# Pacing the sums in smaller transfers, gating a retention head slice by slice, and splitting one gate's weight earlier

## The chip, the cores and the metric

The kernel runs on one core of one Trainium2 chip. The metric is device time in microseconds for one execution of the whole program; lower is better. Before: 2340.71 us, the median of three timed runs. TensorE is the matrix engine, VectorE (DVE in the profile) and ScalarE (ACT) work on its results and on the weights, GpSimd (POOL) does small things and issues one kind of DMA, SyncE (SP) issues the loads of weights.

## What is computed

The reference is a trunk of two layers (512 frames, width 1024, float32). Cut to what matters:

```python
for i in range(DEPTH):                                   # 2 layers
    h = rmsnorm(x, norm1_g[i])
    z = h @ w_in[i] + b_in[i]                            # mLSTM q,k,v,o,i,f; retention q,k,v,g; gates gm, gr
    hm  = mlstm(conv_swish(q), conv_swish(k), v, i, f)   # 4 heads of 256
    y_m = sigmoid(o) * head_layernorm(hm)
    hr  = retention(rope(rq), rope(rk), rv)              # 4 heads, keys of 256, values of 512
    y_r = silu(rg) * head_layernorm(hr)
    merged = sigmoid(gm) * (y_m @ w_bm[i]) + sigmoid(gr) * (y_r @ w_br[i])
    x = x + merged @ w_out[i]
    x = x + square(relu(rmsnorm(x) @ w_ff1[i] + b_ff1[i])) @ w_ff2[i] + b_ff2[i]
    x = x + sigmoid(rmsnorm(x) @ w_pe_gate[i]) * (p[i] @ w_pe[i])
return rmsnorm(x, final_g)
```

## The kernel before, in words

**Units.** All products with weights are a list of 290 units, written out by hand (`unit_list`), 145 for each layer. A T8 unit makes 128 output columns from all eight 128-row blocks of the input (24 matmuls, the weight tile is 128x1024). A V unit is a quarter of a value projection. A PAIR unit makes 256 columns and a WIDE unit 1024 by a seven-product scheme (P1 to P7, in place of eight) on quarter matrices. Layer by layer the list goes: mLSTM (T8 and V), WIDE `rv0`, four T8 of `w_bm`, PAIRs of `rqk0` (tiles `r0brq`, `r0brk`) and of the gate `gm`, WIDE `rw0` and `rv2`, PAIRs of `rqk2`, T8 of `w_br`, WIDE `rw2`, PAIRs of the gate `gr` (tiles `gr0` to `gr3`) between T8 of `w_br`, T8 of `w_out`, then the channel block: T8 of `w_ff1` with PAIRs of `w_ff2` (tiles `o00` to `o33`: block, then pair), then the embedding. Every float32 product is three matmuls: each operand is split into a high part (fp32r) and the low rest, and high by high, low by high and high by low are added.

**Weights.** SyncE loads a weight tile `wr` (four raw buffers, `RAWS`); ScalarE copies it to the high half `wh` and VectorE subtracts to get the low half `wl` (`split`, lines 284 and 285). `prep_next` does this two pieces ahead of use (`LOOK`), and `in_order` keeps the order of the loads and that of the splits. The instructions of each engine run in one fixed order, which a scheduler derives from the program's order and from priorities (`tc.high_priority`). Of a PAIR's weight the pieces are A (`B11`, `t1`), C (`B22`, `t3`), B (`B21`) and D; B's second half is formed on VectorE (line 428) and D from B (line 431).

**Sums.** The seven-product scheme needs sums of weight blocks: `t1` and `t3`, and for WIDE units `t2` and `t4`. They are made ahead of time by DMA alone: GpSimd issues a copy DRAM to DRAM and later an adding one (`step`, line 332). `steps` is the list of all of them. A step has 256 KB in a group of PAIRs (`wpairs`) and 512 KB in a WIDE group (`wwide`: `rv0`, `rw0`, `rv2`, `rw2`). The pace is a credit that starts at -12: each unit adds `SHARE * t - load` (`TIME`: 5.45 and 1.5 for a T8 or V, 9.9 and 3.9 for a PAIR, 5.45 and 2.7 for each two turns of a WIDE), a step takes `STEP` (twice that for 512 KB), and `pace` issues one step where the credit is not negative. Every DMA of a step waits for the matmul that was last in the program when it was issued. `pace` is called at the start of each unit, in the middle of a T8, after each product of a PAIR, and at each second turn of a WIDE unit. A group must be made before its pieces are loaded.

**Retention heads.** `r_attend` runs `attend` (four row slices of 128 frames, each evacuated by ScalarE into `num`, line 801), then the statistics of all four slices (`head_stats`, lines 809 and 810), then `hv`, the power of the variance, on GpSimd (lines 1104 and 1105). `r_gate` of a slice scales the gate by `hv` on ScalarE (line 1143) and multiplies it with the centred slice on VectorE (line 1144). Heads 0 and 2 are gated in the middle of the WIDE unit that makes the gates (`r_gates`); heads 1 and 3 in a loop over the four slices after `r_attend`. `r_out` transposes the gated head on TensorE (line 821, tiles `ot`). `flush` runs the last product (P4) of the PAIR before, which is put off (`later`); P4 writes into the bank that P7's eviction (line 577) frees.

**The mLSTM gate.** `gm_tile(c)` makes a tile of the gate `gm` in a T8 unit (tiles `bgm`); `gm_tile(2)`, weight columns from `CGM + 2 * P`, stands between the output gates of head 0 and the transposes of head 0. `xn_tile` forms the normalised input (`xn`, a high and a low half) for all later units, the first of which is the T8 of head 2 (tiles `m2z`).

Of the kernel before, what the change touches and what calls it, by code (L numbers as in the profile page):

```python
# [35 lines left out]
F32 = mybir.dt.float32  # L36
# [6 lines left out]
P = 128  # L43
T = 512
NT = T // P
# [58 lines left out]
TURNS += [(x, u) for x in ("P7", "P3", "P4") for u in range(2)]  # L104
HALVES = [(WIDE[x][0], u) for x, u in TURNS]

STEP, SHARE = 1.13, 0.73
TIME = {"PAIR": (9.9, 3.9), "WIDE": (5.45, 2.7)}


# [9 lines left out]
def is_wide(g):  # L120
    return g[1][:2] in ("rv", "rw")
# [112 lines left out]
def build(ctx, tc, ins, out):  # L234
# [74 lines left out]
    def flat(a):  # L309
        return a.rearrange("a p q -> (a p q)").rearrange("(r w) -> r w", r=P)  # L310

    def sum_steps():

        out = []
        for g, v in groups().items():
            n = 2 if is_wide(g) else len(v)
            for p in range(n + 1):
                out += [(g, x, 0, p) for x in ("t1", "t3") if p < n]
                out += [(g, x, 1, p - 1) for x in ("t1", "t3") if p]
            out += [(g, x, a, p) for x in LATE if x in MADE_OF(g) for a in range(2) for p in range(n)]  # L320
        return out

    steps = sum_steps()
    made = {}

    def step():
        g, x, a, p = steps[at["step"]]
        at["step"] += 1
        at["credit"] -= STEP * (2 if is_wide(g) else 1)
        made[g, p] = made.get((g, p), 0) + 1  # L330
        kw = {"accum_op": OP.add} if a else {}
        dma = gp.dma_start(flat(block(g, x)[p:p + 1]), flat(block(g, MADE[x][a])[p:p + 1]), max_dma_last_dim=4096,
                           **kw)

        tc.add_manual_dep(dma.ins, cur["mm"].ins.name, SYNC, reason="pace of the sums")

# [3 lines left out]

    def tick(kind=None):
        t, load = TIME.get(kind, (5.45, 1.5))
        at["credit"] += SHARE * t - load
        pace()

    def next_unit():
# [47 lines left out]
    def prep_next():  # L394
# [15 lines left out]
        if gates:  # L410
            z = out_[0]
            gp.memset(z.bitcast(F32), 0.0)
            z = z.rearrange("p (k g c) -> p k g c", g=4, c=32)
            split(r[:, 0:64].rearrange("p (k g c) -> p k g c", g=2, c=H), z[:, :, 0:2, 0:H], z[:, :, 2:4, 0:H])
        elif x == 0:
            with tc.high_priority(AHEAD if n < 10 and units[n][0] == "V" else 0):
                for c in halves(n):
                    in_order("prep", *split(r[:, c], *[a[:, c] for a in out_]))
        else:
            in_order("prep", *split(r[:, :w], *out_))  # L420
# [96 lines left out]
    def run_wide(name, act, done, mid=None):  # L517
# [4 lines left out]
        for x, u in TURNS:  # L522
# [23 lines left out]
            if u:  # L546
                for t in range(2):
                    done(x, t, bank[b][t])

    def ahead():  # L550

        return tc.high_priority(AHEAD)

    def pair_tiles(name, act, consume, y=None):

        y = y or [tmp(f"{name}y{d}") for d in range(2)]
        a, b = slice(0, S), slice(S, T)

        def done(x, o):
            with ahead():  # L560
                evict(x, o)
            if x == "P4":
                consume(y)

        def evict(x, o):
            if x == "P1":
                ac.activation(y[0][:, b], o, AF.Copy)
            elif x == "P5":
                ac.activation(y[1][:, a], o, AF.Copy)
            elif x == "P2":  # L570
                ve.tensor_tensor(y[0][:, b], o, y[0][:, b], OP.add)
            elif x == "P6":
                ac.activation(y[1][:, b], o, AF.Copy)
            elif x == "P3":
                ve.tensor_tensor(y[1][:, b], o, y[1][:, b], OP.add)
            elif x == "P7":
                ve.tensor_tensor(y[1][:, a], o, y[1][:, a], OP.add)
            else:
                ac.activation(y[0][:, a], o, AF.Copy)

        run_pair(name, act, done)
# [209 lines left out]
            off += w  # L791
        return ph, pl, offs

    def attend(nm, pt, vh, vl, c0, n, num):
        ph, pl, offs = pt
        for j in range(NT):
            o = ps(f"{nm}a{j}")
# [3 lines left out]
            ac.activation(num[:, j, :], o[:, :n], AF.Copy)  # L801
            if j == 0:
                flush()

    def head_stats(nm, num, dv):
        st = cols.tile([P, NT, 6], F32, name=f"{nm}st", tag="st")
# [130 lines left out]
    for i in range(L):  # L937
# [157 lines left out]
            nc.scalar.dma_start(dg, ins["decay"][h])  # L1095
            return scores(f"l{i}r{h}", qk[0], qk[1], qk[2], qk[3], lambda a: dg[:, 0:T - a * P])

        def r_attend(h, pt, vv):
            nm = f"l{i}r{h}"
            num = cur["low"].tile([P, NT, 512], F32, name=f"{nm}num", tag="num")  # L1100
            attend(nm, pt, vv[0], vv[1], 0, 512, num)
            mv = head_stats(nm, num, 512)
            hv = cols.tile([P, NT], F32, name=f"{nm}hv", tag="hv")
            gp.tensor_scalar(hv, mv[:, :, 1], EPS, None, OP.add)
            gp.tensor_tensor(hv, hv, nhalf, OP.pow)
            return num, mv, hv

        def r_gates(h, norm, mid):

# [221 lines left out]
        g = r_gates(0, num, lambda: rv_split(vv))  # L1331
        yr = acts(cur["br"], f"l{i}yr0")
        r_out(0, num[0], yr)
        num = r_attend(1, pt, vv)
        for j in range(NT):
            r_gate(num, g, j)
        vv = rv_vals(2, lambda: r_out(1, num[0], yr))
        qk = r_qk(2)

# [14 lines left out]
        g = r_gates(2, num, lambda: rv_split(vv))  # L1354
        yr = acts(cur["br"], f"l{i}yr1")
        r_out(2, num[0], yr)
        num = r_attend(3, pt, vv)
        for j in range(NT):
            r_gate(num, g, j)
        mh, ml = [], []  # L1360
        gr = {}

        def gr_gates(p):
            def consume(g):
                for d in range(2):
                    ac.activation(g[d], g[d], AF.Sigmoid, bias=bcol(i, "bgr", 2 * p + d), scale=SIGN[d])
                    gr[2 * p + d] = g[d]

            pair_tiles(f"l{i}gr{p}", xs, consume)

        gr_gates(0)
        r_out(3, num[0], yr)
        for c in range(KT):
            if c and c % 2 == 0:
# [355 lines left out]
```

## Time and profile before

| what | value |
|---|---|
| timed runs, median (lowest to highest) | 2340.71 us (2340.2 to 2340.83) |
| the profiled execution | 2335.82 us |
| its span, first to last instruction | 2334.1 us |
| granted TensorE clock, mean | 0.998 |
| busy: TensorE, VectorE, ScalarE, GpSimd | 99%, 73%, 52%, 17% |
| DMA: mean rate; share of queue q0 (GpSimd's, the sums) and of q1 (SyncE's, the loads) | 181 GB/s; 26.0% and 34.0% |

The durations in the profile belong to the one profiled execution. Its own time is 1.7 us over its span and 4.9 us under the median of the timed runs. A row of waits tells which engine stood idle before which line and what released it; a small wait on TensorE moves everything behind it.

### The profile page before, as it was taken

The page shows a single profiled execution, that of the slowest core. Times are in us where ns is not written, and L with a number is a line of the kernel's source. Part 1 is how long each engine was busy: PE and PEld are TensorE (multiplying, and loading weights), DVE is VectorE, ACT ScalarE, POOL GpSimd, SP SyncE. Part 2 cuts the span into 40 slices and gives each one's busy share as a digit, 9 for nine tenths or more (in the row PEclk, how much of TensorE's full clock was granted, in tenths as well). Part 3 has the DMA queues.
Part 4 walks back from the last instruction along what each step waited for, and adds up shares of the span by engine and source line. Part 5 has one row for each costly group of instructions (what it writes and reads, how often), then busy time and mean ns, then how long its engine had stood idle before and what let it go on. Part 6 is the DMA issues. An engine that isn't in the chain of part 4 may idle for free.

```text
span 2334.1 us, 34266 instructions
## 1 busy us (share of the span) xinstructions
PE 2311.7 (99%) x12992; PEld 2019.8 (87%) x12992; DVE 1709.6 (73%) x2594; ACT 1217.2 (52%) x1731; POOL 398.3 (17%) x618
## 2 busy tenths in 40 slices
PE   9999999999999999999999999999999999999998
PEld 8888889888888888899888888988888988998997
DVE  7878767886765577678778777778767656776785
ACT  6756544644554445445557564445446445445464
POOL 3122111111124312111422222200000020000012
PEclk9999999999999999999999999999999999999999
DMA  6667877777788787787786668945444443433441
GB/s 219 165 178 194 233 218 207 211 223 217 203 243 250 190 229 185 213 221 195 209 229 165 163 162 244 257 148 174 143 148 153 149 154 98 127 109 95 136 122 55
DMA packets 152328, 422.13 MB, mean 181 GB/s; under 512 B 19089, under 2 KB 22545, under 8 KB 152161
## 3 DMA queue, kind: packets, MB, share of 16 engines
q1 hardware_dynamic: 97504, 257.99, 34.0%
q0 software_dynamic: 39248, 134.51, 26.0%
q10 hardware_dynamic: 15408, 27.43, 3.4%
q8 instruction: 102, 1.67, 0.3%
q14 instruction: 66, 0.53, 0.1%
HBM read 400.97 MB, written 140.51 MB: 232 GB/s over the span
## 4 chain that ended last, share of the span: by engine, by line
PE 87%; DVE 5%; issue 3%; DMA 2%; ACT 1%; POOL 1%; SPq 0%; DVEq 0%; ACTq 0%; POOLq 0%
PE l1f L449 2%; PE l0f L449 2%; PE l0f L450 2%; PE l1f L450 2%; PE l1f L451 2%; PE l0f L451 2%; PE l0br L449 1%; PE l1br L449 1%; PE l0br L450 1%; PE l1br L450 1%; PE l1br L451 1%; PE l0br L451 1%; DMA wr<-s8t 1%; PE l0pg L449 1%; PE l1bm L449 1%
## 5 line engine op out<-in xcount | busy, mean ns | idle before, releaser
L284 ACT ACTIVATE wh<-wr 128x1024 fp32r<-128x1024 f32 (+1 forms) x223 | 231.3, 1044 | 261.3 <-issue 62.7
L285 DVE TENSOR_TENSOR wl<-wr,wh 128x1024 fp32r<-128x1024 f32 (+1 forms) x221 | 272.4, 1234 | 49.6 <-ACT wh L284 49.3
L284 ACT ACTIVATE wh_B<-wr 128x1024 fp32r<-128x1024 f32 x108 | 114.4, 1060 | 175.9 <-PE l0br L450 15.7
L285 DVE TENSOR_TENSOR wl_B<-wr,wh_B 128x1024 fp32r<-128x1024 f32 x108 | 131.9, 1222 | 53.8 <-ACT wh_B L284 53.5
L449 PE MATMUL l1f<-l1n2h,wh 128*128 128x512 f32 x256 | 99.8, 390 | 0.0
L449 PE MATMUL l0f<-l0n2h,wh 128*128 128x512 f32 x256 | 99.8, 390 | 0.0
L451 PE MATMUL l1f<-l1n2h,wl 128*128 128x512 f32 x256 | 99.7, 389 | 0.0
L451 PE MATMUL l0f<-l0n2h,wl 128*128 128x512 f32 x256 | 99.6, 389 | 0.0
L450 PE MATMUL l0f<-l0n2l,wh 128*128 128x512 f32 x256 | 99.6, 389 | 0.0
L450 PE MATMUL l1f<-l1n2l,wh 128*128 128x512 f32 x256 | 99.6, 389 | 0.0
L284 ACT ACTIVATE wh_t<-wr 128x1024 fp32r<-128x1024 f32 x56 | 59.4, 1060 | 72.0 <-PE l0g2va L544 6.0
L284 ACT ACTIVATE wh_C<-wr 128x1024 fp32r<-128x1024 f32 x60 | 63.3, 1056 | 64.3 <-issue 8.5
L284 ACT ACTIVATE wh_D<-wr 128x512 fp32r<-128x512 f32 x60 | 37.9, 632 | 112.6 <-DVE wr L431 59.3
L285 DVE TENSOR_TENSOR wl_t<-wr,wh_t 128x1024 fp32r<-128x1024 f32 x56 | 68.2, 1220 | 27.9 <-ACT wh_t L284 27.3
L285 DVE TENSOR_TENSOR wl_C<-wr,wh_C 128x1024 fp32r<-128x1024 f32 x60 | 74.9, 1248 | 17.9 <-ACT wh_C L284 17.2
L284 ACT ACTIVATE wh_A<-wr 128x1024 fp32r<-128x1024 f32 x60 | 63.1, 1052 | 39.3 <-PE l0f L450 6.7
L285 DVE TENSOR_TENSOR wl_A<-wr,wh_A 128x1024 fp32r<-128x1024 f32 x60 | 73.3, 1221 | 11.1 <-ACT wh_A L284 10.4
L660 POOL TENSOR_TENSOR l1n3sum<-l1n3sum,l1n3sq 128x512 f32<-128x512 f32 x6 | 9.2, 1529 | 330.5 <-ACT l1n3sum L652 309.4
L285 DVE TENSOR_TENSOR wl_D<-wr,wh_D 128x512 fp32r<-128x512 f32 x60 | 41.4, 690 | 25.0 <-ACT wh_D L284 23.9
L451 PEld LDWEIGHTS l1f<-l1n2h,wl 128*128 128x128 f32 x256 | 48.1, 188 | 10.2
L451 PEld LDWEIGHTS l0f<-l0n2h,wl 128*128 128x128 f32 x256 | 48.1, 188 | 10.1
L450 PEld LDWEIGHTS l1f<-l1n2l,wh 128*128 128x128 f32 x256 | 48.1, 188 | 9.8
(4990 smaller groups left out, 8330.1 us busy)
## 6 DMA issues: line engine op xcount, KB each, us to landing
wr<-wstream SPq DMA_DIRECT2D x219, 512.0 KB, 4.5
wr<-wpairs SPq DMA_DIRECT2D x180, 256.0 KB, 3.5
wr<-wwide SPq DMA_DIRECT2D x48, 512.0 KB, 4.4
s3t<-wwide POOLq DMA_DIRECT2D x12, 512.0 KB, 6.2
s6t<-wwide POOLq DMA_DIRECT2D x12, 512.0 KB, 6.0
s15t<-wwide POOLq DMA_DIRECT2D x12, 512.0 KB, 5.8
s18t<-wwide POOLq DMA_DIRECT2D x12, 512.0 KB, 6.0
s0t<-wwide POOLq DMA_DIRECT2D x10, 512.0 KB, 7.4
```

What stands on the lines that cost most here:

```text
L284: a = ac.activation(hi_ap, src, AF.Copy)
L285: return a, ve.tensor_sub(lo_ap, src, hi_ap.bitcast(F32))
L449: te.matmul(o, sh, mh, start=first, stop=False)
L450: te.matmul(o, sh, ml, start=False, stop=False)
L451: cur["mm"] = te.matmul(o, sl, mh, start=False, stop=last)
L660: (add or gp).tensor_tensor(self.sum, self.sum, sq, OP.add)
```

## The change

Three things, in one diff.

- A step of a WIDE group is split in two: 256 KB each (`piece`), and each takes `STEP`. `SHARE` becomes 0.75 up to the WIDE unit `rw2` of layer 0 (`rush`) and 0.63 (`LATER`) from there on. `run_wide` calls `pace` after every turn as well.
- `attend` calls a function after each slice: the slice's statistics, its addition and power on GpSimd (columns of `hv` one by one) and, for heads 1 and 3, the gating of the slice before. The last slice of head 1 is gated after `r_attend`; that of head 3 after product P2 of the PAIR `gr0` (`then`).
- The splits of the weight of `gm_tile(2)` (`SOON`), in both layers, are issued with `high_priority(AHEAD)`.

```diff
-STEP, SHARE = 1.13, 0.73
+SOON = ("w_in", 0, CGM + 2 * P)
+STEP, SHARE, LATER = 1.13, 0.75, 0.63
...
+    def piece(g, x, p, q):
+        b = block(g, x)[p:p + 1]
+        if q is None:
+            return flat(b)
+        return b.rearrange("a p q -> (a p q)").rearrange("(h r w) -> h r w", h=2, r=P)[q]
+
     def sum_steps():
         out = []
         for g, v in groups().items():
-            n = 2 if is_wide(g) else len(v)
+            ps_ = [(p, q) for p in range(2) for q in range(2)] if is_wide(g) else list(range(len(v)))
+            n = len(ps_)
             for p in range(n + 1):
-                out += [(g, x, 0, p) for x in ("t1", "t3") if p < n]
-                out += [(g, x, 1, p - 1) for x in ("t1", "t3") if p]
-            out += [(g, x, a, p) for x in LATE if x in MADE_OF(g) for a in range(2) for p in range(n)]
+                out += [(g, x, 0, ps_[p]) for x in ("t1", "t3") if p < n]
+                out += [(g, x, 1, ps_[p - 1]) for x in ("t1", "t3") if p]
+            out += [(g, x, a, p) for x in LATE if x in MADE_OF(g) for a in range(2) for p in ps_]
         return out
     steps = sum_steps()
+    rush = units.index(("WIDE", (0, "rw2"), 0))
...
         g, x, a, p = steps[at["step"]]
         at["step"] += 1
-        at["credit"] -= STEP * (2 if is_wide(g) else 1)
-        made[g, p] = made.get((g, p), 0) + 1
+        at["credit"] -= STEP
         kw = {"accum_op": OP.add} if a else {}
-        dma = gp.dma_start(flat(block(g, x)[p:p + 1]), flat(block(g, MADE[x][a])[p:p + 1]), max_dma_last_dim=4096,
-                           **kw)
+        p, q = p if is_wide(g) else (p, None)
+        made[g, p] = made.get((g, p), 0) + (0.5 if is_wide(g) else 1)
+        dma = gp.dma_start(piece(g, x, p, q), piece(g, MADE[x][a], p, q), max_dma_last_dim=4096, **kw)
...
-        at["credit"] += SHARE * t - load
+        at["credit"] += (SHARE if at["unit"] <= rush else LATER) * t - load
         pace()
...
-            with tc.high_priority(AHEAD if n < 10 and units[n][0] == "V" else 0):
+            with tc.high_priority(AHEAD if n < 10 and units[n][0] == "V" or units[n][1:] == SOON else 0):
...
     (run_wide, at the end of each turn)
+            pace()
...
-    def pair_tiles(name, act, consume, y=None):
+    def pair_tiles(name, act, consume, y=None, then=None):
...
                 evict(x, o)
+            if then and x == "P2":
+                then()
...
-    def attend(nm, pt, vh, vl, c0, n, num):
+    def attend(nm, pt, vh, vl, c0, n, num, each=None):
...
             if j == 0:
                 flush()
+            if each:
+                each(j)
...
-        def r_attend(h, pt, vv):
+        def r_attend(h, pt, vv, g=None):
             num = cur["low"].tile([P, NT, 512], F32, name=f"{nm}num", tag="num")
-            attend(nm, pt, vv[0], vv[1], 0, 512, num)
-            mv = head_stats(nm, num, 512)
+            st = cols.tile([P, NT, 6], F32, name=f"{nm}st", tag="st")
+            mv = cols.tile([P, NT, 2], F32, name=f"{nm}mv", tag="mv")
             hv = cols.tile([P, NT], F32, name=f"{nm}hv", tag="hv")
-            gp.tensor_scalar(hv, mv[:, :, 1], EPS, None, OP.add)
-            gp.tensor_tensor(hv, hv, nhalf, OP.pow)
-            return num, mv, hv
+            norm = num, mv, hv
+
+            def each(j):
+                ve.bn_stats(st[:, j, :], num[:, j, :])
+                ve.bn_aggr(mv[:, j, :], st[:, j, :])
+                c = hv[:, j:j + 1]
+                gp.tensor_scalar(c, mv[:, j, 1:2], EPS, None, OP.add)
+                gp.tensor_tensor(c, c, nhalf[:, 0:1], OP.pow)
+                if g and j:
+                    r_gate(norm, g, j - 1)
+
+            attend(nm, pt, vv[0], vv[1], 0, 512, num, each)
+            return norm
...
-        num = r_attend(1, pt, vv)
-        for j in range(NT):
-            r_gate(num, g, j)
+        num = r_attend(1, pt, vv, g)
+        r_gate(num, g, NT - 1)
...
-        num = r_attend(3, pt, vv)
-        for j in range(NT):
-            r_gate(num, g, j)
+        num = r_attend(3, pt, vv, g)
...
-        gr_gates(0)
+        gr_gates(0, lambda: r_gate(num, g, NT - 1))
         r_out(3, num[0], yr)
```

More of the change, by code (lines that the diff above doesn't have):

```diff
@@ L1356, in build, with gr_gates @@
         r_out(2, num[0], yr)
-        num = r_attend(3, pt, vv)
-        for j in range(NT):
-            r_gate(num, g, j)
+        num = r_attend(3, pt, vv, g)
         mh, ml = [], []
         gr = {}
-        def gr_gates(p):
+        def gr_gates(p, then=None):
             def consume(g):
@@ L1367, in consume @@
                     gr[2 * p + d] = g[d]
-            pair_tiles(f"l{i}gr{p}", xs, consume)
-        gr_gates(0)
+            pair_tiles(f"l{i}gr{p}", xs, consume, then=then)
+        gr_gates(0, lambda: r_gate(num, g, NT - 1))
         r_out(3, num[0], yr)
```

## The prediction

> **What bounds the kernel now.** I read the page first, then who waited for whom on TensorE, then the chain that ended last, and then the DMA view, the timelines and the busy times of the stretches in which TensorE stood still.
>
> ```profile
> span 2334.1 us, 34266 instructions
> PE 2311.7 (99%) x12992; PEld 2019.8 (87%) x12992; DVE 1709.6 (73%) x2594; ACT 1217.2 (52%) x1731; POOL 398.3 (17%) x618
> ```
>
> TensorE is busy in 2311.7 of 2334.1 us. The change touches no matmul, so all that it can win is idle time of TensorE, and most of that has names:
>
> ```profile
> PE l0o02a L499 <- DVE l0x L1451: 2.5, 1, 2.5
> PE l0r0brqa L499 <- DVE l0r0brqy L577: 2.1, 1, 2.1
> PE l0gr0a L499 <- DVE l0gr0y L577: 1.4, 1, 1.4
> ...
> PE l1bgm L451 <- DVE wl L285: 1.0, 1, 1.0
> ...
> PE l0bgm L451 <- DVE wl L285: 1.0, 1, 1.0
> ...
> PE l1gr0a L499 <- DVE l1gr0y L577: 1.0, 1, 1.0
> ...
> PE l1m2z L450 <- DVE l1xnl L285: 0.3, 1, 0.3
> PE l0o02a L501 <- DVE wl_B L285: 0.2, 1, 0.2
> ```
>
> Columns: who waited for whom, us in total, times, longest. The three parts of the change meet these waits: l0o02 (2.5 + 0.2) and l0r0brq (2.1) stand where sums and weight loads share the DMA engines; l0gr0 and l1gr0 (1.4 + 1.0) come right after the retention head 3; l0bgm and l1bgm (1.0 + 1.0) wait for the low half of one gate's weight. Together 9.2 us; that is the ceiling of the gain.
>
> **Part 1, sums in 256 KB and the pace.** In layer 0's first channel block the chain runs through a slow load, while seven sums of 512 KB were issued within 29 us (stretch 827 to 856):
>
> ```profile
> 837.24 8.35 DMA wr<-s8t
> ```
>
> ```profile
> q0 software_dynamic: 1088, 3.93, 58.4%
> ...
> s12t<-wwide POOLq DMA_DIRECT2D x7, 512.0 KB, 5.5
> ```
>
> Price of one 256 KB of sums: 58.4% of 29 us is 16.9 us of all DMA engines for seven times 512 KB, so 1.2 us. Why seven came: before, a T8 unit earns 0.73 x 5.45 - 1.5 = 2.48 of credit and has two places to issue; two sums of 256 KB cost 2.26, so 0.22 is left over per unit, and by counting the units forward from the code I find a credit of 5.2 when this block's first PAIR unit begins. Each of the PAIR's places then issues until the credit is gone. After the change LATER holds here: a T8 earns 1.93, less than two sums cost, so nothing piles up; a PAIR earns 0.63 x 9.9 - 3.9 = 2.34, that is two sums of 256 KB where the first PAIR had four of 512 KB. I take the whole wait off: **-2.7 us** (bounds 0 and -2.7).
>
> The same count in layer 0's retention stage goes the other way. With STEP now charged per 256 KB and SHARE 0.75, a V unit earns 2.59 and has one place to issue (1.13), so each of the eight V units leaves 1.46; each of some 26 T8 units leaves 0.33: 11.7 + 8.6, once the -12 of the start is paid. Credit reaches 20 at the first WIDE unit (rv0), against -1.7 before. That unit now has 21 places (14 turns, 7 ticks), earns 7 x 1.39 and spends 21 x 1.13: every place fires, 21 sums of 256 KB against eight (four of 512 KB) before. About 8 of credit is left at the first two PAIRs (r0brq, r0brk): 7 and then 6 sums of 256 KB. This is the place of the 2.1 us wait, so the question is whether 13 small ones hurt less than the large ones there. The trace has an almost exact answer, because layer 1 runs the same code at the same place with 256 KB sums and a large credit. First layer 0, then layer 1, VectorE's timeline, then the DMA view of layer 1 (1466 to 1486) and that stretch's busy times:
>
> ```profile
> 319.01 0.69 DVE L428 TENSOR_TENSOR wr<-wr,wr 128x512 f32<-128x512 f32 x1 [4.57 <-DMA wr<-wpairs]
> ```
>
> ```profile
> 1475.15 0.69 DVE L428 TENSOR_TENSOR wr<-wr,wr 128x512 f32<-128x512 f32 x1 [1.98 <-DMA wr<-wpairs]
> ```
>
> ```profile
> q0 software_dynamic: 935, 3.08, 62.9%
> ...
> s22t<-wpairs POOLq DMA_DIRECT2D x7, 256.0 KB, 6.9
> s23t<-wpairs POOLq DMA_DIRECT2D x5, 256.0 KB, 8.7
> wr<-wstream SPq DMA_DIRECT2D x2, 512.0 KB, 8.2
> ```
>
> ```profile
> 1466.00:1486.00 20.00, 20.00 (x168) 19.88 (x167) 14.90 (x22) 10.28 (x16) 7.27 (x12) 1.00 0.99 277
> ```
>
> In layer 0 VectorE stood 4.57 us before L428 and so evacuated the bank that TensorE wanted late. In layer 1 twelve 256 KB sums were issued in 20 us, the DMA engines were 0.99 busy, VectorE stood 1.98 us, and TensorE lost nothing (20.00 of 20). The new layer 0 is nearest to this row. The margin is small, so I take **-1.6** of the 2.1 (bounds: -2.1; and +2.1 if thirteen sums double the wait).
>
> The rv0 stage has no such twin:
>
> ```profile
> 246.00:286.00 40.00, 40.00 (x182) 32.69 (x181) 33.81 (x50) 18.48 (x23) 7.49 (x11) 1.00 0.79 243
> ```
>
> ```profile
> wr<-wwide SPq DMA_DIRECT2D x3, 512.0 KB, 5.1
> ```
>
> Its DMA share is 0.79 of 40 us; 13 more sums at 1.2 us are 15.6 us, or 0.39: 1.18 in all. The sums are over-subscribed there, but they are due far later; what counts is the weight loads. They take 5.1 us to land now and took 8.2 us at a DMA share of 0.99. Twelve are wanted in 40 us, one per 3.3 us, so with four raw buffers one load and its splits may take 13 us and still be in time. I take +0.4 here; below, a rival has the full price. After that, in layer 1, the sums run on for some 30 units longer by my count, at two per PAIR; the PAIRs of layer 0 had three such sums or more with no wait but those named: 0.
>
> The extra issues cost GpSimd time alone: 112 wide sums become 224. A 256 KB issue took 0.78 us (the POOL row in part 2), so this is at most 87 us over some 1800, on an engine that is 17% busy: 0.
>
> The Trainium skill (DMA: Bandwidth & Descriptors, section "Anatomy of one DMA — SWDGE (gpsimd) path") speaks against the split: each transfer carries about 2.0 us that do not shrink with its size, beside its bytes. By it a 256 KB sum is an estimated 2.6 us, not 1.2, the 21 sums of rv0 would fill 55 us of a stage of 40, and the sum below would have the price of the second rival. The layer 1 rows (12 sums in 20 us, TensorE at 20.00) disagree where transfers overlap; no run here shows it beside WIDE loads.
>
> **Part 2, head statistics and gating by slices.**
>
> ```profile
> 646.19 3.13 DVE L1144 SCALAR_TENSOR_TENSOR l0r3num<-l0r3num,l0r3mv,l0g2y 128x512 f32<-128x512 f32 x4 [3.23 <-ACT l0g2y L1143]
> ...
> 652.17 0.42 DVE L577 TENSOR_TENSOR l0gr0y<-l0gr0a,l0gr0y 128x256 f32<-128x256 f32 x1
> ```
>
> ```profile
> 643.19 0.78 POOL L332 DMA_DIRECT2D s7t<-wpairs  x1 [0.56 <-DVE l0r3mv L810]
> 644.04 0.23 POOL L1104 TENSOR_SCALAR l0r3hv<-l0r3mv 128x4 f32<-128x4 f32 x1
> 644.35 1.04 POOL L1105 TENSOR_TENSOR l0r3hv<-l0r3hv,nhalf 128x4 f32<-128x4 f32 x1
> ```
>
> Now all four slices wait for the last slice's statistics: GpSimd's issue of a sum (0.78), the addition (0.23), the power (1.04) and ScalarE's scaling. VectorE stands 3.23 us and then gates for 3.13 us; the eviction L577, for which TensorE waits 1.4 us, comes behind that. After: slices 0 to 2 are gated inside the attention, and slice 3 after the eviction of P2, when its power is long done. VectorE then has up to 3.23 + 3 x 0.78 = 5.6 us less ahead of L577, more than 1.4. Added: a power for each slice. The nearest small power is
>
> ```profile
> L689 POOL TENSOR_TENSOR l1n41rc<-l1n41ms,nhalf x2: 558/558/559, 2324.3 to 2324.8; 128x1 f32<-128x1 f32 x2
> ```
>
> so a slice costs GpSimd at most 0.23 + 0.56 = 0.8 us, and a head 3.2 instead of 1.3. What queues behind a slice on ScalarE and VectorE, both in order, is the next slice's eviction and the splits of gr0's weights; TensorE has the rest of the attention as cover. I take **-2.4** for both layers (bounds -2.4 and +3.0: three slices that each wait 0.8 us and meet an issue of 0.78 would stand VectorE 4.7 us instead of 3.23, 1.5 more in each layer). For heads 0, 1 and 2 no wait stands behind the gating now: 0.
>
> **Part 3, one gate's weight first.** Moving the split up removes 1.0 us in each layer. But VectorE is the bound of that stretch:
>
> ```profile
> 91.00:127.00 36.00, 34.97 (x178) 29.40 (x177) 34.73 (x65) 26.06 (x43) 8.28 (x12) 1.00 0.60 149
> ```
>
> ```profile
> 125.59 1.29 DVE L285 TENSOR_TENSOR l0xnl<-l0xnr,l0xnh 128x512 fp32r<-128x512 f32 x2
> ```
>
> VectorE is busy in 34.73 of 36 us and ends that run with the last two low halves of xn, which the next T8 (m2z) needs; in layer 1 TensorE waits for that very split already (l1m2z, 0.3). The split that is moved up pushes all else on VectorE back by its 1.2 us until its old place and takes nothing away. So TensorE gets to m2z 1.0 us earlier and waits there 1.0 us longer. What is late next is xnl. I take **-0.2** for both layers (bounds -2.0 and +0.5).
>
> **Sum.** -2.7 - 1.6 + 0.4 - 2.4 - 0.2 = -6.5 us. The profiled execution (2335.8 us, its span 2334.1) would be 2329.3; it lies 4.9 us under the median of the timed runs, 2340.7, so the forecast is **2334.2**. A difference of 0.2% (4.7 us, so under 2336.0 or over 2345.4) is about what a measurement of this kernel can tell from no change.
>
> **Rivals.** *The wait only moves* (chance 0.25): r0brq keeps its 2.1 us, because 13 sums of 256 KB carry more bytes than those before, the slices leave VectorE half of its wait (-1.2), and rv0 costs 1. Then -2.7 - 1.2 + 1 = -2.9: 2337.8, no measurable change. For it speaks the small margin in layer 1 (L428 still stood 1.98 us); against it that TensorE lost nothing there. This holds also the case that the scheduler leaves slice 3's gating, or the sums, much where they were.
>
> *The WIDE stage starves* (0.15, slower). When rv0's loads land after 8.2 us, and high and low half are split in
>
> ```profile
> L284 ACT ACTIVATE wh<-wr 128x1024 fp32r<-128x1024 f32 (+1 forms) x223 | 231.3, 1044 | 261.3 <-issue 62.7
> L285 DVE TENSOR_TENSOR wl<-wr,wh 128x1024 fp32r<-128x1024 f32 (+1 forms) x221 | 272.4, 1234 | 49.6 <-ACT wh L284 49.3
> ```
>
> 1.0 + 1.2 us before the buffer is free, a buffer turns in 10.4 us. With four in flight that is 2.6 us a load and nothing is lost; with two, 5.2 us, 1.9 too slow, 23 us over twelve loads, and the whole comes to 2334.2 + 23 = 2357. The point from which it decides is 10.4 / 3.3 = 3.2 loads in flight; one of the four buffers is held in part of the stage for the sum of t4, which speaks for it, the 5.1 us landing now against it.
>
> **How the numbers follow.** My forecast has 0.60: all its outcomes, from the ceiling of 9.2 down to a gain of 4.7, are faster. The first rival, 0.25, is the same; the second, 0.15, slower. The range begins a little beyond the ceiling, 2330, as waits under the view's threshold may go too; above it takes in the first rival and a third of the second's price (2334.2 + 8): 2342. What stays outside is mostly starvation in full.
>
> **What would show it.** Right: no l0o02a and l0gr0a rows among TensorE's waits; in rv0 (246 to 286) a DMA share above 0.95 with TensorE at 40 of 40; L428 near 318 us standing 2 to 3 us; bgm's rows gone, and an l0m2z and a longer l1m2z row in their place, of about 1 us. Wrong: l0r0va or bm rows with waits of over 1 us would be the starvation; l0gr0a rows that stay, behind L1144 with idle time before it, would refute part 2; bgm gone without m2z growing would refute part 3.

## The result, and the profile after

| | before | after |
|---|---|---|
| timed runs, median (lowest to highest) | 2340.71 us (2340.2 to 2343.21) | 2330.15 us (2328.28 to 2331.78) |
| ratio of the two | | 0.9952, interval 0.9937 to 0.9967 |
| the profiled execution | 2335.82 us | 2331.78 us |

The change makes the kernel 0.5% faster: 10.6 us by the medians. The two profiled executions differ by 4.0 us only. That gap between what one profile shows and what the timed runs show is the subject of most of the experiments. The page splits the 4.0 us: TensorE stands idle 5.6 us less (16.8 us of the span, 22.4 before), and its busy time is 1.6 us longer for the same matmuls.

The page of after, its span and busy times. TensorE's count of matmuls is as before; GpSimd has 160 instructions more, the added sums and the powers of single slices:

```profile
span 2330.1 us, 34559 instructions
PE 2313.3 (99%) x12992; PEld 2021.4 (87%) x12992; DVE 1709.6 (73%) x2594; ACT 1217.6 (52%) x1731; POOL 497.2 (21%) x778
```

Who waited for whom on TensorE, after (us in total, times, longest). Gone are l0o02a (2.5 and 0.2) and the two bgm rows. l0r0brqa stands at 1.7, the gr0 rows stand at 0.8 and 0.6 and wait for ScalarE now, and l1m2z has grown from 0.3 to 0.8:

```profile
PE l0r0brqa L509 <- DVE l0r0brqy L590: 1.7, 1, 1.7
...
PE l0gr0a L509 <- ACT l0gr0y L580: 0.8, 1, 0.8
PE l1m2z L460 <- DVE l1xnl L286: 0.8, 1, 0.8
PE l1gr0a L509 <- ACT l1gr0y L580: 0.6, 1, 0.6
```

The busy times of the stretch of the WIDE unit rv0 and of the first PAIRs behind it, and the sums and loads issued in the first (DMA view, columns: count, size, median us from issue to landing):

```profile
246.00:284.00 38.00, 38.00 (x170) 30.95 (x169) 31.96 (x45) 16.22 (x19) 16.29 (x26) 1.00 1.01 305
...
306.00:327.00 21.00, 19.33 (x161) 19.09 (x160) 14.15 (x20) 10.27 (x16) 8.45 (x13) 1.00 0.98 239
```

```profile
s3t<-wwide POOLq DMA_DIRECT2D x11, 256.0 KB, 6.1
s3t<-s3t POOLq DMA_DIRECT2D x8, 256.0 KB, 6.4
...
wr<-wstream SPq DMA_DIRECT2D x4, 512.0 KB, 8.4
wr<-wwide SPq DMA_DIRECT2D x3, 512.0 KB, 6.7
```

19 sums went out in rv0, the DMA engines were full (1.01), and TensorE lost nothing (38.00 of 38). The page of the Trainium skill that the prediction weighed (DMA: Bandwidth & Descriptors, "Anatomy of one DMA — SWDGE (gpsimd) path": some 2.0 us of each transfer that its size does not shrink) is not borne out as a cost of 19 transfers one after the other: at 2.6 us each they would have taken 49 us of a stage of 38. The loads of 512 KB there took 6.7 to 8.4 us to land, as slow as the second rival supposed, and TensorE still did not wait.

In the first PAIR, VectorE stood before the same addition for 4.13 us, 4.57 before; the prediction had looked for 2 to 3:

```profile
316.90 0.69 DVE L438 TENSOR_TENSOR wr<-wr,wr 128x512 f32<-128x512 f32 x1 [4.13 <-DMA wr<-wpairs]
```

### The profile page after: what moved, and what is told of

Its sections match the earlier page's. It is cut to its first block, busy times and chain, and to the rows that moved or that the text cites. A ratio compares the mean times of both kernels' runs of the same rounds, so it can differ in the third digit from the quotient of the medians.

```text
span 2330.1 us, 34559 instructions
## 1 busy us (share of the span) xinstructions
PE 2313.3 (99%) x12992; PEld 2021.4 (87%) x12992; DVE 1709.6 (73%) x2594; ACT 1217.6 (52%) x1731; POOL 497.2 (21%) x778
## 4 chain that ended last, share of the span: by engine, by line
PE 90%; DVE 5%; issue 2%; ACT 1%; DMA 1%; POOL 1%; ACTq 0%; DVEq 0%; POOLq 0%; SPq 0%
PE l0f L459 3%; PE l1f L459 3%; PE l1f L460 2%; PE l0f L460 2%; PE l0f L461 2%; PE l1f L461 2%; PE l0br L459 1%; PE l1br L459 1%; PE l1br L460 1%; PE l1br L461 1%; PE l0br L460 1%; PE l0br L461 1%; PE l0pg L459 1%; PE l0bm L459 1%; PE l0pg L460 1%
## 5 line engine op out<-in xcount | busy, mean ns | idle before, releaser
L460 PEld LDWEIGHTS l0f<-l0n2l,wh 128*128 128x128 f32 x256 | 48.1, 188 | 9.8
```

Source lines behind the costliest of these rows:

```text
L460: te.matmul(o, sh, ml, start=False, stop=False)
```

## The experiments

Times are medians with lowest and highest; ratios are against the kernel before, run on the same chip in the same session (32, 35, 17, 11 and 15 runs of it in the five sessions, medians 2337.8 to 2339.2, single runs from 2331.5 to 2348.2). "Clock" is the mean granted clock, averaged over the timed runs of a kernel; it was 0.9975 over all 110 runs of the kernel before.

| run | what it is | us | ratio (interval) | clock |
|---|---|---|---|---|
| a1_before_again | before, unchanged | 2336.46 (2334.07 to 2344.28) | 0.9997 (0.9987 to 1.0007) | 0.9975 |
| a2_sums_only | part 1 | 2331.59 (2331.16 to 2333.0) | 0.9976 (0.9966 to 0.9986) | 0.9982 |
| a3_slices_only | part 2 | 2338.71 (2334.46 to 2344.36) | 0.9998 (0.9987 to 1.0009) | 0.9976 |
| a4_split_only | part 3 | 2339.51 (2335.98 to 2341.51) | 0.9999 (0.9991 to 1.0008) | 0.9975 |
| b1_cap_l0 | credit cut, layer 0 | 2336.16 (2333.89 to 2338.51) | 0.9992 (0.9983 to 1.0000) | 0.9977 |
| b2_cap_l1 | credit cut, layer 1 | 2336.45 (2332.97 to 2342.84) | 0.9997 (0.9986 to 1.0007) | 0.9977 |
| b3_cap_both | both | 2335.41 (2331.98 to 2338.0) | 0.9985 (0.9977 to 0.9994) | 0.9976 |
| b4_size_nolater | 256 KB without the slower pace | 2337.34 (2332.8 to 2341.08) | 0.9995 (0.9985 to 1.0006) | 0.9978 |
| c1_after_again | the whole change | 2328.87 (2326.74 to 2330.65) | 0.9958 (0.9942 to 0.9973) | 0.9980 |
| c2_sums_again | part 1 | 2329.41 (2328.67 to 2330.96) | 0.9961 (0.9946 to 0.9976) | 0.9980 |
| c3_sums_slices | parts 1 and 2 | 2328.25 (2324.89 to 2332.07) | 0.9953 (0.9937 to 0.997) | 0.9980 |
| c4_pace_512 | the pace with 512 KB | 2335.87 (2333.5 to 2337.79) | 0.999 (0.9979 to 1.0) | 0.9973 |
| d1_gates_two | slices 2 and 3 gated late | 2330.69 (2327.6 to 2331.86) | 0.9963 (0.9951 to 0.9975) | 0.9982 |
| d2_gates_few | d1, fewer sums at r0brq | 2331.07 (2329.11 to 2331.46) | 0.9965 (0.9953 to 0.9976) | 0.9980 |
| d3_stall_short | 16 short stalls put in | 2366.02 (2362.71 to 2367.14) | 1.0114 (1.0101 to 1.0128) | 0.9982 |
| d4_stall_long | 8 long stalls put in | 2378.02 (2376.78 to 2379.12) | 1.0168 (1.0155 to 1.0181) | 0.9935 |
| e1_spare_only | a 16-byte tile added | 2342.96 (2341.68 to 2343.59) | 1.0019 (1.0009 to 1.0028) | 0.9982 |
| e2_gates_behind | d1, ordered | 2330.52 (2329.41 to 2331.28) | 0.9966 (0.9954 to 0.9979) | 0.9982 |

### Which part wins

The expectations name the theories that they weigh. The question of the first four runs was which part wins, and whether the waits that the prediction named are what is won.

The kernel before once more, and each part alone: part 1 is the hunks of `STEP, SHARE, LATER`, `piece`, `sum_steps`, `step`, `tick` and `run_wide`; part 2 those of `attend`, `r_attend`, `pair_tiles` and `gr_gates`; part 3 this one.

```diff
-            with tc.high_priority(AHEAD if n < 10 and units[n][0] == "V" else 0):
+            with tc.high_priority(AHEAD if n < 10 and units[n][0] == "V" or units[n][1:] == SOON else 0):
```

a1_before_again: 

> The kernel of before, unchanged, profiled a second time. Theory A (the trace carries the gain): its profile repeats the first one within 1 us, waits of 2.5 us at l0o02a and 2.1 us at l0r0brqa among them, and the time between 2340 and 2341 has some other source than TensorE's waits. Theory B (the first profile was a lucky execution): this one has a span of about 2338 us, and the difference is either in longer waits behind DMA (l0o02a, l0r0brqa) or in TensorE's rate: the PAIR units o11 to o13 and o21 to o23 of layer 0, which took 9.5 to 9.7 us there, take 9.9.

a2_sums_only: 

> Part 1 alone (256 KB sums, new pace). Theory A: l0o02a's waits (2.7 us in the view, 3.4 with the restart) go, l0r0brqa keeps 1.7 us, rv0 costs nothing: 3.5 to 4 us less than before. Theory B (sums collide more in most executions than in the profiled one of before): 6 to 8 us less, most of the whole gain of 10.6.

a3_slices_only: 

> Part 2 alone (statistics and gating by slices). Theory A: the waits behind L577 (1.4 and 1.0 us) are replaced by waits of 0.8 and 0.6 us for ScalarE's eviction of P1, so 1.0 us less than before. Rival: all 2.4 us go, because the new waits come from the sums that GpSimd issues in between under the new pace; then gr0a has no row among TensorE's waits.

a4_split_only: 

> Part 3 alone (one gate's split first). My prediction: 0.2 us less, the 1.0 us comes back at m2z in both layers. Rival (from the trace of after): bgm's 1.2 us go in both layers and only 0.3 to 0.5 us come back at m2z, so 1.6 us less; VectorE has then closed its 0.9 us of idle time before L815, which the split's old place caused.

Part 1 alone has half of the gain or more (0.24% here, 0.39% in c2), and its eight runs lie within 1.9 us of each other where those of the kernel before spread over 10. Parts 2 and 3 alone are no different from before. Four readings of the traces bear on this.

In the profile of a1 there is no l0o02a row at all; its l0r0brqa row is

```profile
PE l0r0brqa L499 <- DVE l0r0brqy L577: 1.8, 1, 1.8
```

So the 2.7 us that the prediction took off for l0o02 belonged to one execution: the same program had no such wait in the next. TensorE's busy time is 2313.6 us in a1, against 2311.7 in the first profile of the same program and 2313.3 in after. The first profile was a short one in this respect, and the 1.6 us of busy time that after seems to add are not shown to come from the change.

In the profiles of part 1 alone there is no bgm row either. VectorE's timeline in the kernel before, then in a2, shows the split in question 0.84 us earlier, and TensorE comes to these products 0.74 us later (110.07 us, 109.33 before), so that the split is done 0.6 us before it is needed and not 1.0 after. The same 0.6 us stand in b4, c2 and c3, which have 256 KB sums; c4, which keeps 512 KB, still waits 0.7. What in the smaller sums brings it about was not looked into.

```profile
109.71 1.20 DVE L285 TENSOR_TENSOR wl<-wr,wh 128x1024 fp32r<-128x1024 f32 x1
```

```profile
108.87 1.19 DVE L285 TENSOR_TENSOR wl<-wr,wh 128x1024 fp32r<-128x1024 f32 x1
```

Part 3 alone (a4) took the bgm waits away as well (1.0 us in each layer) and paid for it at l1m2z, but less than the prediction said: 0.5 us more than before in layer 1 and nothing in layer 0. Its profile also had 1.0 us before layer 1's second head (0.3 in before, 0.6 in a1); b1, without part 3, had 1.1 there, so this cannot be put down to the part:

```profile
PE l1m1z L450 <- ACT l1gem L908: 1.0, 1, 1.0
...
PE l1m2z L451 <- DVE l1xnl L286: 0.8, 1, 0.8
```

Part 2 alone (a3) has l0gr0a at 0.8, behind ScalarE, in place of 1.4 behind VectorE; in layer 1 it wins nothing (0.6 and 0.5 in place of 1.0).

### Size or pace

The credit cut to the income of one unit, with 512 KB kept (b1 for the units from 67 on in layer 0, b2 from 146 on, b3 from 67 to the end):

```diff
         at["credit"] += SHARE * t - load
+        if 67 <= at["unit"] < 146:
+            at["credit"] = min(at["credit"], SHARE * t - load)
```

and part 1 without its slower second pace:

```diff
-STEP, SHARE, LATER = 1.13, 0.75, 0.63
+STEP, SHARE, LATER = 1.13, 0.75, 0.75
```

b1_cap_l0: 

> The kernel of before, with 512 KB sums and the old pace, but from the PAIRs of gr in layer 0 to the end of that layer the credit is cut to one unit's income. The first PAIR of the first channel block then issues two sums of 512 KB instead of four. Theory ff0 (the time that part 1 wins is lost at that burst, more in most executions than in the profiled ones): 5 to 8 us less than before. Theory L1 (it is lost at layer 1's first two PAIRs of rqk0, 15 sums of 256 KB in 19 us, which this kernel keeps): 0 to 2 us less.

b2_cap_l1: 

> The same cut in layer 1 alone: its first two PAIRs of rqk0 issue three sums each instead of seven and eight or nine; layer 0's burst stays. Theory ff0: 0 to 1 us less than before. Theory L1: 4 to 8 us less.

b3_cap_both: 

> The cut in both places, transfers still of 512 KB. If the bursts are what part 1 wins: as part 1 alone, 7 to 8 us less than before, so the size of a transfer does not matter. If the size matters by itself: under half of that.

b4_size_nolater: 

> Part 1 alone, but without the slower second pace: 256 KB sums, the extra place after each WIDE turn, and 0.75 to the end. Credit piles up again: the first two PAIRs of the first channel block issue 7 and 5 sums of 256 KB, layer 1's rv0 21. If bursts of any size cost: 3 to 7 us more than part 1 alone. If only 512 KB transfers in a burst cost: the same as part 1 alone, within 1 us.

Taking the bursts out while the transfers keep 512 KB wins 0.15% (b3, some 3.5 us), and neither place alone has the 4 us or more that its theory asked for (b1, b2). The smaller transfers at the old rate win nothing that can be told (b4): bursts of 256 KB cost as well. Then the full change, part 1 again, parts 1 and 2, and the pace alone:

```diff
-STEP, SHARE = 1.13, 0.73
+STEP, SHARE, LATER = 1.13, 0.75, 0.63
...
-        at["credit"] += SHARE * t - load
+        at["credit"] += (SHARE if at["unit"] <= rush else LATER) * t - load
```

with `pace()` after every turn of a WIDE unit as well.

c1_after_again: 

> The changed kernel once more, on the chip of the next three. Theory A (the slower second pace with no bursts is nearly the whole gain; slices and split add 0 to 2 us): a ratio of 0.995 to 0.998, a median of 2329 to 2333, at most 2 us under the sums alone. Theory C (the three parts help one another, for instance because the later pace leaves room that the slices then use): 3 us or more under the sums alone. TensorE's waits as before: l0gr0a and l1gr0a behind ScalarE's P1 copy 0.6 to 0.8, l0r0brqa 0.4 to 1.7, no bgm rows, no l0o02a row.

c2_sums_again: 

> Part 1 alone again (256 KB sums, a step within the wide units, the slower second pace). Theory A: ratio 0.997 to 0.998, 2331 to 2334, spread of the runs below 3 us. If the earlier 0.9976 was the luck of one session: 0.999 or more and a spread of 8 us like the kernel before.

c3_sums_slices: 

> Parts 1 and 2 without the early weight split. Since part 1 alone already had no wait at the bgm products (VectorE came to that split 0.84 us sooner), theory A says the split adds nothing on top: the same time as the full change within 1 us. Theory C (the split counts): 1.5 us or more over the full change, with bgm rows of about 1 us back in TensorE's waits.

c4_pace_512: 

> Only the pace of part 1: transfers of 512 KB as before, credit 0.75 early and 0.63 later, one try for a sum after every product group of a wide unit. Theory P (the pace wins, the size does not): 0.9970 to 0.9985, within 1.5 us of the sums alone, spread below 4 us. Theory S (the 256 KB pieces win because a load behind a sum waits for half the bytes): 0.999 to 1.000, with waits of 1 us or more at l0r0brqa, l0o02a or in layer 1's first stage.

On one chip, part 1 (2329.41), parts 1 and 2 (2328.25) and all three (2328.87) cannot be told apart: parts 2 and 3 add nothing that the runs resolve. Size and pace have to come together: 0.9990 and 0.9995 apart, 0.9961 and 0.9976 together. TensorE's longest wait in c4 (pace, no size), in b4 (size, no pace) and the same place in c2 (both; it has no l0o02a row):

```profile
PE l0r0brqa L500 <- DVE l0r0brqy L579: 3.3, 1, 3.3
```

```profile
PE l0o02a L508 <- DVE l0x L1465: 2.2, 1, 2.2
```

```profile
PE l0r0brqa L508 <- DVE l0r0brqy L589: 0.6, 1, 0.6
```

The size cures r0brq. The copies of the sums landed in 9.1 us there in c4 and in 5.8 in c2 (stretch 306 to 320 and 306 to 318), and the two loads of weights beside them in 7.7 and 5.0:

```profile
s4t<-wwide POOLq DMA_DIRECT2D x2, 512.0 KB, 9.1
...
wr<-wpairs SPq DMA_DIRECT2D x2, 256.0 KB, 7.7
```

```profile
s4t<-wwide POOLq DMA_DIRECT2D x8, 256.0 KB, 5.8
wr<-wpairs SPq DMA_DIRECT2D x2, 256.0 KB, 5.0
```

TensorE's wait follows the landing of these loads from profile to profile: 0.6 us at 5.0, 1.0 at 5.4, 1.7 at 6.1 (after), 2.1 at 6.5 (before), 2.6 at 7.0 (b2), 3.3 at 7.7. So it is the late load for which TensorE stands, through VectorE.

The pace matters in the channel block, where b4 still issued 15 sums of 256 KB between 827 and 856 (before: seven of 512 KB). Each half alone leaves one long stall, in the one profile that each has. Against c2 the spans of c4 and b4 are 4.9 and 5.9 us longer; the waits that differ account for 3.4 in c4 (2.7 at r0brq, 0.7 at bgm) and for 2.7 in b4 (2.2 at l0o02a, 0.5 at l0o32a). What else is in b4 shows in the granted clock.

### A long stall can cost more than its length

The busy times of b4 in steps of 1 us around that stall (the column before the last two is the granted clock):

```profile
854.00:855.00 1.00, 0.00 (x0) 0.00 (x0) 1.00 (x3) 0.00 (x0) 0.00 (x0) 1.00 0.19 66
...
856.00:857.00 1.00, 1.00 (x7) 1.00 (x8) 1.00 (x2) 0.29 (x1) 0.00 (x0) 0.73 0.57 119
857.00:858.00 1.00, 1.00 (x7) 1.00 (x7) 1.00 (x2) 0.00 (x0) 0.00 (x0) 0.50 0.95 344
858.00:859.00 1.00, 1.00 (x6) 1.00 (x6) 1.00 (x3) 0.80 (x1) 0.33 (x1) 0.50 0.82 152
859.00:860.00 1.00, 1.00 (x7) 1.00 (x6) 0.81 (x2) 0.26 (x1) 0.17 (x1) 0.56 0.85 287
860.00:861.00 1.00, 1.00 (x11) 1.00 (x10) 0.96 (x3) 0.00 (x0) 0.11 (x1) 1.00 1.00 369
```

After the stall TensorE worked at half its clock for 3.4 us (7 matmuls a microsecond, not 11), which cost 1.7 us on top of the 2.2. Of the nine stalls between 1.9 and 3.3 us in the profiles of sessions one to three and of the kernel before, three were followed by such a stretch (b4, and b1 and b2 at r0brq); no single stall under 1.9 us was, ahead of the program's end. To price it by itself, waits for GpSimd were put into layer 1's channel block of the changed kernel: 16 times for one power, or 8 times for two (cut).

```diff
+            if at["seen"] % 4 == 0 and at["seen"] <= 32:     # d3: % 2
+                for r in range(2):                           # d3: range(1)
+                    stall_ = gp.tensor_tensor(spare, spare, nhalf, OP.pow)
...
+                stall = stall_
...
+                f_ = te.matmul(o, wh[:, s], act[0][k], start=True, stop=False)
+                tc.add_manual_dep(f_.ins, stall.ins.name, SYNC, reason="stall")
```

d3_stall_short: 

> The changed kernel with 16 stalls of TensorE put in on purpose, at every second T8 unit of layer 1's ff1: GpSimd does one pow of 128x4 (1.04 us) after the matmul before, and the next matmul waits for it. Both theories: 16 stalls of 1.2 to 1.4 us, 19 to 22 us over the changed kernel, no stretch of the granted clock below 1.00 there, mean clock 0.998.

d4_stall_long: 

> The same with 8 stalls of two pows (2.3 to 2.5 us) at every fourth T8 unit: the same pows, half the hand-overs. Theory N (a stall costs its length): 18 to 20 us over the changed kernel, 1 to 2 us under the 16 short ones, mean clock 0.998. Theory K (a stall of over about 2 us halves the granted clock for 3.4 us in some of its cases, 1.7 us each): 2 to 6 of the 8 stalls are followed by such a stretch, 3 to 10 us more, so level with the short ones or up to 9 us over them, mean clock 0.996 to 0.997, and runs that scatter by several us.

TensorE's waits in d3, then in d4:

```profile
PE l1f L481 <- POOL spare L474: 18.7, 16, 1.4
```

```profile
PE l1f L481 <- POOL spare L474: 23.3, 8, 3.0
```

The long ones came out at 2.6 to 3.0 us, longer than expected. The waits differ by 4.6 us, the medians by 12.0. Five of the eight long stalls were followed by a half clock, three times for 3.4 us and twice for 6.8; one of the latter:

```profile
2232.00:2234.00 2.00, 1.03 (x3) 0.84 (x4) 0.05 (x1) 0.07 (x1) 0.91 (x1) 0.55 0.40 104
2234.00:2236.00 2.00, 2.00 (x6) 1.61 (x5) 0.00 (x0) 0.00 (x0) 0.00 (x0) 0.50 0.41 158
2236.00:2238.00 2.00, 2.00 (x6) 1.52 (x6) 0.00 (x0) 0.00 (x0) 0.00 (x0) 0.50 0.04 8
2238.00:2240.00 2.00, 2.00 (x8) 1.57 (x7) 0.00 (x0) 0.00 (x0) 0.00 (x0) 0.74 0.00 0
```

The sixteen short stalls had none. Theory K holds: the shortfalls of clock in the 2-us rows of d4's channel block add up to 12.0 us, and the mean clock falls to 0.9935. The Trainium skill (TensorE: Matmul & The Clock Gate, section "HAM oscillation — how this bites in real kernels") gives the rule that idle gaps must not exceed about 3.4 us; here 2.07 us were enough, and 3.3 us once did nothing. That the same page lets the window of the gate run free fits the traces, in which the position of a stall decides. The half clock begins on a grid of 3.413 us in each execution: d4's six stretches (starts from 1955.73 to 2368.74 us, the one at the program's end included) lie whole multiples of it apart, and so do the two of b1, of b2 and of b4. Laid on that grid, c4's stall of 3.3 us falls on two steps, and b1's of 2.07 us on one (the second column is the length, the third TensorE's busy time):

```profile
317.55:320.96 3.41, 1.61 (x14) 1.40 (x12) 1.02 (x3) 0.77 (x2) 0.54 (x1) 1.00 0.97 330
320.96:324.37 3.41, 1.89 (x15) 1.89 (x16) 3.29 (x5) 0.00 (x0) 0.00 (x0) 1.00 0.72 238
```

```profile
318.64:322.05 3.41, 1.34 (x12) 1.21 (x11) 3.38 (x6) 0.38 (x1) 0.00 (x0) 1.00 0.81 138
322.05:325.46 3.41, 3.41 (x19) 3.41 (x18) 2.63 (x5) 1.89 (x4) 0.00 (x0) 0.50 0.60 191
```

Ahead of the program's end, all eight steps at full clock with 2.07 us or more of idle TensorE were followed by half clock, and none with 1.86 us or less. The end is different: there TensorE has few and short matmuls between waits of 1.2 us at most, and in all twenty profiles the clock is 0.50 over the last 7 to 11 us, in c1 from 1.3 us after a wait of 1.0. So short stalls that lie close together can cost clock too.

### What the stalled kernels had besides, and what part 2 left

Both stalled kernels were longer than their stalls and the clock explain, by some 13 to 17 us. e1 is the changed kernel with only their scratch tile:

```diff
+    spare = cpool.tile([P, NT], F32, name="spare")
+    gp.memset(spare, 2.0)
```

e1_spare_only: 

> The changed kernel with the scratch tile of 128 x 4 numbers (16 bytes a partition, set once at the start) that the two kernels with stalls have, and no stall. Theory L (the tile moves every later tile of its memory by 16 bytes and the T8 matmuls read slower for it): 13 to 16 us over the changed kernel, 0.16 us in each of some 90 T8 units, with TensorE's waits as they were. Rival (the instructions of the stalls do it): 2329 to 2331, as the changed kernel.

The tile alone costs 13 us (2342.96; d3 and d4 lie 23.1 and 35.1 over it, for some 21.9 and 24.6 us that the matmuls start later at the stalls and, in d4, the 12.0 of clock; this leaves 1.2 us over and 1.5 us under). The matmuls of layer 0's ff1 in after and in e1 (view of one tile: minimum, median, maximum ns):

```profile
L459 PE MATMUL l0f<-l0n2h,wh x256: 389/389/486, 770.1 to 1065.2; 128*128 128x512 f32 x128
```

```profile
L461 PE MATMUL l0f<-l0n2h,wh x256: 391/396/477, 771.2 to 1071.0; 128*128 128x512 f32 x128
```

By their starts these matmuls are 6 ns further apart (232 ns, 226 in c1), some 0.15 us in a T8 unit. Layer 1's ff1 has none of it (226 in both). Over all tiles the matmuls start 12.8 us later in e1 than in c1, which is the whole cost. Theory L's first half is shown (the tile does it, not the stalls); that it is the address of later tiles is the likely reading but was not measured.

Then the waits that part 2 left. In after, ScalarE's timeline at head 3 of layer 0 has the gating of slice 2 ahead of P1's copy, and that gating waits for its power:

```profile
642.58 0.72 ACT L1168 ACTIVATE l0g2y<-l0g2y,l0r3hv 128x512 f32<-128x512 f32 x1 [1.06 <-POOL l0r3hv L1126]
643.21 0.36 ACT L580 ACTIVATE l0gr0y<-l0gr0a 128x256 f32<-128x256 f32 x1
```

d1 moves the gating of slice 2 behind P2, beside slice 3's; d2 also holds the first PAIR of layer 0 to three sums; e2 makes the gating depend on P1's copy.

```diff
-        gr_gates(0, lambda: r_gate(num, g, NT - 1))
+        gr_gates(0, lambda: [r_gate(num, g, j, cur["p1"]) for j in (NT - 2, NT - 1)])   # d1, d2: without cur["p1"]
```

d1_gates_two: 

> The changed kernel, with the gating of slices 2 and 3 of head 3 both put behind the first product of the gr gates (slices 0 and 1 stay between the attention's slices), so that ScalarE copies P1 out before it waits for slice 2's pow. If part 2's lost gain is that in-order wait of ScalarE: the l0gr0a and l1gr0a rows (0.8 and 0.6 us) go and the time falls by 1.0 to 1.5 us against the changed kernel's 2329 to 2330, ratio about 0.9953. Rival: the wait moves to the first transpose of head 3's output (l0r3ot, l1r3ot), 0.5 us or more each, and the time stays within 0.5 us.

d2_gates_few: 

> As the one before, and in the first PAIR unit of layer 0 (its r0brq) at most 3 sums of 256 KB are issued instead of 7. If the loads of the weights there are late because sums share the DMA engines: the l0r0brqa row (1.0 to 1.7 us) falls below 0.5, another 1 us off, 2327 to 2328. Rival: the sums not issued there run in the next two PAIR units and the wait moves there (l0r0brka or l0bgm2a rows of 0.5 us or more), no gain.

e2_gates_behind: 

> The changed kernel with the gating of slices 2 and 3 of head 3 held behind ScalarE's copy of P1 by a dependency. If ScalarE's wait for slice 2's pow is what keeps P6 waiting: no l0gr0a or l1gr0a row of over 0.3 us, 1.0 to 1.4 us less in the profile than the changed kernel beside it, about 2328 to 2329 timed. Rival: l0r3ot or l1r3ot wait 0.5 us or more for slice 3's gating, and the time stays.

In d1 the scheduler put ScalarE's instructions in the same order as in the changed kernel, so the waits stayed (0.8 and 0.5) and the run says nothing of the theory. d2 has 0.9 us at l0r0brqa beside c1's 1.0: with five sums issued in that stretch (306 to 318) instead of eight the wait is still there, as the loads landed in 5.2 us, 5.4 in c1. One profile of each, at a place that varies from 0.5 to 1.7 with part 1, does not show more. In e2 the copy does come first, and the wait changes engine; VectorE now gates slice 2 ahead of the addition for which TensorE waits:

```profile
PE l1gr0a L509 <- DVE l1gr0y L590: 0.6, 1, 0.6
PE l0gr0a L509 <- DVE l0gr0y L590: 0.6, 1, 0.6
```

Neither expectation of e2 was right, and none of the three beats the changed kernel.

## Why the prediction was right in its direction and wrong in its size

The direction was right. 2330.15 lies at the very edge of the range of 2330 to 2342 (the ratio of 0.9952 on 2340.71 gives 2329.5, just outside), and the forecast of 2334.2 was 4 us too high. Point by point:

- **The step that failed** is the last of the sum: "it lies 4.9 us under the median of the timed runs, 2340.7, so the forecast is 2334.2". It took for granted that the profile's distance from the median stays. In after the profile lies 1.6 us over the median, so 6.5 us of the result come from this step. The 4.9 us were partly chance: the first profile of before has little busy time (2311.7 us, 2313.6 in a1), and the five timed runs beside it were long ones (2340.2 to 2343.2; the 110 later runs have a median of 2338.2).
- **The sum against the profile.** -6.5 us from 2335.8 gives 2329.3; after's profile is 2331.78, so 4.0 us were won there and not 6.5. That 2329.3 is near the timed median of 2330.15 is luck: the profile came out 2.5 us above it, and the median 1.6 below the profile. In TensorE's waits the terms are -2.7 for l0o02 (as taken), -0.4 for r0brq (taken at -1.6), -1.0 for gr0 (-2.4), -1.5 for bgm less l1m2z (-0.2) and nothing in rv0 (+0.4): -5.6, and the busy time gave 1.6 back.
- **Why single runs scatter** is only argued. The waits behind DMA vary from profile to profile, as the next point shows. Before, single runs lay between 2331.5 and 2348.2; with part 1 alone, within 2.3 us of each other in a session. But c3, which has part 1 too, spread over 7.2 us in six runs, so part 1 does not by itself make the runs alike.
- **Part 1** (taken at -2.7, -1.6 and +0.4) was sized from one execution. l0o02a was 2.5 in one profile and absent in the next; r0brq was 1.8 to 2.6 in the seven profiles with 512 KB and the old pace at that place, and 1.7, 1.0, 1.0, 0.8 and 0.6 in the five of part 1 alone or with the others. In after's own profile the loads landed in 6.1 us, 6.5 before, so 0.4 us went and not 1.6. Timed, part 1 is worth 5.6 us (a2) to 9.1 us (c2) by its ratios. It also took away the bgm waits, which the prediction had given to part 3.
- **The clock** was left out of the prediction, and part of part 1's gain may be there. The mean clock rose from 0.9975 to between 0.9980 and 0.9986; 0.0007 of 2335 us is an estimated 1.6 us. The mean needs care: the half clock at the program's end alone makes it 0.9977 to 0.9986 in the profiles. A run listed at 0.997 or less has more than that: 49 of the 110 runs of before are, 2.3 us longer on average than the other 61, and none of the 29 runs of after, a2, c1, c2 and c3. The profile of before had both long stalls and no half clock after either, so nothing in it showed the price.
- **Part 2** (-2.4) is at most about half of that: the gr0 rows went from 1.4 and 1.0 to 0.8 and 0.6. "GpSimd at most 0.8 us a slice" held for two of the four slices of head 3 (1.0 and 1.2 us for the others, the third behind the issue of a sum of 0.89). The prediction looked for the queue on VectorE alone; ScalarE, in order too, stood 1.06 us before slice 2's gating with P1's copy behind it. Alone, the part is not measurable (0.9998).
- **Part 3** (-0.2) came out as forecast in time (0.9999 alone), but not by the way told: TensorE did not wait 1.0 us longer at m2z in each layer, but 0.5 in layer 1 and not at all in layer 0, and where the rest of the 2.0 us went is not shown. In the change it meets a wait that part 1 has already removed.
- **The WIDE stage starves**: refuted, 38.00 of 38 at a DMA share of 1.01. The credit count was near: 19 sums seen in rv0, 21 predicted.
- **The wait only moves**: true in part for part 2 (from VectorE to ScalarE) and part 3 (0.5 of 2.0 us), not for part 1.

Open: of 8.7 us between the timed means of before and of part 1 (2338.2 and 2329.5 in the third session) the spans of the two profiles differ by 6.4, and the clock is an estimated 1.6. The first of these profiles is not typical of its kernel, so this is a rough account. What is left, and why a2 and c2 differ by 2 us between two chips, were not settled.

## What to carry to other kernels

A wait behind a DMA in one profile is a sample: ask in how many executions it comes, from a second profile or from the spread of the timed runs, before you price its removal, and do not carry the profile's distance from the median over to the new kernel. Where TensorE is the bound, rank its stalls by length first, since one of over 2 us may also cost 1.7 us of clock; two of 1 us did not in the middle of this program, but waits of 1 us close together did at its end. When one engine's queue is relieved, look for the next engine that takes the same instructions in order before the wait counts as gone.

## What the runs showed of the hardware

- A TensorE stall of 2.07 us can be followed by 3.4 us at half clock; of 17 stalls between 1.9 and 3.3 us in all profiles, eight were. The half clock begins on a grid of 3.413 us, and before the program's end it followed every step with 2.07 us or more of idle TensorE and none with 1.86 or less.
- With the DMA engines at a share of 1.01 for 38 us, loads of 512 KB still landed (in 6.7 to 8.4 us) in time for TensorE to lose nothing.
- 16 bytes a partition more of allocated SBUF put the 128x512 matmuls of some stages some 6 ns further apart, 13 us in the whole kernel. After and before have the same median there (389 ns), so this plays no part in the change.
